# Where feed-forward weights begin in their buffers: eight places instead of one

## The chip, the cores and the metric

The kernel runs on one core of one Trainium2 chip. Its five engines (TensorE, VectorE, ScalarE, GpSimd and SyncE) run side by side and meet at semaphores. The metric is the time of one execution on the device, in microseconds; three executions before the change took 817.57, 817.77 and 818.57 us, with a median of 817.77 us.

## The reference

One encoder block on 512 tokens of width 1024, all in float32: three sub-layers, each with an RMSNorm before and after it and a residual.

```python
h = rms_norm(x, g_mix_pre);  proj = h @ w_in            # 1024 x 3080
...                                                     # two groups of 8 heads, joined, @ w_out
x = x + rms_norm(mix, g_mix_post)
ca = memory_cross_attention(rms_norm(x, g_mem_pre), rms_norm(mem, g_mem_kv), w_mem_q, w_mem_kv, w_mem_o)
x = x + rms_norm(ca, g_mem_post)
h = rms_norm(x, g_ffn_pre)
g, u = split(h @ w_gate_up)                             # 1024 x 2 * 2816
x = x + rms_norm((silu(g) * u) @ w_down, g_ffn_post)    # 2816 x 1024
```

The feed-forward part at the end is what the change concerns: 512 x 1024 by 1024 x 5632, then 512 x 2816 by 2816 x 1024.

## The kernel before, in words

Every float32 product is made of three matmuls of a rounded type. A matrix is split into `hi`, its rounded value, and `lo`, what the rounding lost, and `mm3` (L142 to L145) adds stationary hi by moving hi (L143), stationary hi by moving lo (L144) and stationary lo by moving hi (L145) in PSUM. The stationary operand is loaded into TensorE by its own instruction (LDWEIGHTS, the rows marked PEld), here 128 columns at a time; the moving operand streams past it, here up to 512 columns at a time.

The weights come in 63 units, listed in order at L200 to L222. `load_unit` (L102) brings one: SyncE issues a DMA into a buffer `raw` (L114, 128 x 1024 elements at a time, three buffers in turn), ScalarE casts it into `hi` (L118), and VectorE subtracts to get `lo` (L125; GpSimd does part of it for early units, L121). `unit` (L135) hands out the next unit and has the one after it loaded ahead. `hi` and `lo` have two buffers each, taken in turn, so the unit after next waits until TensorE has finished with its buffer. A unit is a tile of 128 partitions by `nkb` blocks by `ncol` columns, 8 x 256 or 4 x 512 elements of 4 bytes, 8192 bytes per partition. The opening stage uses the same buffers for `vhi264`, `vlo264` (8 blocks of 264 columns, 8448 bytes) and `vhi256`, `vlo256`. A scheduler orders the work by priorities, which `later` shifts.

The order of the stages is: value columns of the input projection (`v_products`, moving operand `vhi`/`vlo`, stationary `hTh`/`hTl`); the projections and the attention of four head groups; output projection with the keys and values of the memory; cross-attention; `w_mem_o`; and the feed-forward part.

Units 29 to 50 are the gate and up weights, in 11 pairs. There the weights are stationary, 128 columns at a time, and the normalised activations `fh`/`fl` are moving, 512 columns, for the first pair in two pieces of 256 columns. Each pair makes 128 x 512 results in PSUM for two blocks of gate (`ps_a`) and up (`ps_s`); ScalarE and VectorE turn them into `gh` and `gl` (L833 to L836). Units 51 to 62 are the down weights, six for each half of the 1024 output columns. There `gh`/`gl` are stationary and the weights are moving, 512 columns. Unit 56 is the last of the first half; it and unit 62 have two blocks instead of four. The second half's first unit, 57, takes the buffer of unit 55, which the end of the first half uses, so its cast and its subtraction come after that use.

Of the kernel before, what the change touches and what calls it, by code (L numbers as in the profile page):

```python
# [9 lines left out]
F32R = mybir.dt.float32r  # L10
# [4 lines left out]
P = 128  # L15
# [3 lines left out]
KB = D // P  # L19
# [14 lines left out]
def hybrid_block_kernel(  # L34
# [23 lines left out]
    wp = ctx.enter_context(tc.tile_pool(name="wp", bufs=2))  # L58
# [9 lines left out]
    def f32(ap):  # L68
        return ap.bitcast(F32)
# [32 lines left out]
    def load_unit(w, k0, nkb, c0, ncol, dst=None, sizes=None, after=None):  # L102
        u = len(loaded)
        if dst is None:
            hi = wp.tile([P, nkb, ncol], F32R, tag="hi", name=f"hi{u}", bufs=2)
            lo = wp.tile([P, nkb, ncol], F32R, tag="lo", name=f"lo{u}", bufs=2)
        else:
            hi, lo = dst()
        step = nkb if nkb * ncol <= 1024 else 4 if ncol < 512 else 2
        j = 0  # L110
        for n in sizes or [min(step, nkb - k) for k in range(0, nkb, step)]:
            raw = wp.tile([P, n, ncol], F32, tag="raw", name=f"raw{u}_{j}", bufs=3)
            r0 = (k0 + j) * P
            nc.sync.dma_start(  # L114
                raw,
                w[r0 : r0 + n * P, c0 : c0 + ncol].rearrange("(k p) n -> p k n", p=P),
            )
            act.copy(hi[:, j : j + n, :], raw)  # L118
            pk = 0 if j == 0 or not 0 <= u < 24 else 3 if ncol == 256 else 2 if u >= 18 else 0
            if pk:  # L120
                pool.tensor_tensor(  # L121
                    out=lo[:, j : j + pk, :], in0=raw[:, :pk, :], in1=f32(hi[:, j : j + pk, :]), op=ALU.subtract
                )
            if pk < n:
                dve.tensor_tensor(  # L125
                    out=lo[:, j + pk : j + n, :], in0=raw[:, pk:, :], in1=f32(hi[:, j + pk : j + n, :]), op=ALU.subtract
                )
            if after is not None:
                after(hi, lo, j, n)
            j += n  # L130
        loaded.append((hi, lo))
# [3 lines left out]
    def unit(ahead=1):  # L135
        n = used[0]
        used[0] += 1
        while len(loaded) < min(n + 1 + ahead, len(units)):
            load_unit(*units[len(loaded)])
        return loaded[n]  # L140
# [60 lines left out]
    for side in range(2):  # L201
        for g in fox_order if side == 0 else (0, 1):
            c = (0, 1544)[side] + 256 * g
            n = 264 if (side, g) == (0, 1) else 256
# [24 lines left out]
    with tc.tile_pool(name="mix", bufs=1, reuse_waits="tile") as bp:  # L229
# [403 lines left out]
        with later(-5):  # L633
            for half in range(2):
                hi, lo = unit()
# [10 lines left out]
    with tc.tile_pool(name="cross", bufs=1, reuse_waits="tile") as cp:  # L646
# [9 lines left out]
        with later(-115):  # L656
            for c in range(4):
                hi, lo = unit()
# [17 lines left out]
        for half in range(2):  # L676
            hi, lo = unit()
# [19 lines left out]
        for half in range(2):  # L697
            accs = [bank("a"), bank("a")]
            for k0 in (0, 4):
                hi, lo = unit()  # L700
# [15 lines left out]
        for h in range(4):  # L716
            hi, lo = unit()
# [11 lines left out]
            p = cp.tile([P, NT, NMEM], F32, tag="xp", name=f"xp{h}", bufs=2)  # L729
# [63 lines left out]
        for pair in range(2):  # L793
            for half, w in enumerate((w0, w1)):
                for t in (2 * pair, 2 * pair + 1):
                    acc = bank("a")
                    ts = slice(t * P, (t + 1) * P)
                    for k in range(KB):
                        hi, lo = w[k // 4]
# [11 lines left out]
    with tc.tile_pool(name="ffn", bufs=1, reuse_waits="tile") as fp:  # L811
# [30 lines left out]
        for half in range(2):  # L842
# [11 lines left out]
            for k0, n in groups[:4]:  # L854
                hi, lo = unit()
# [81 lines left out]
```

## Time and profile before

| what | value |
|---|---|
| median of three runs | 817.77 us (817.57 to 818.57) |
| the profiled execution | 817.99 us |
| its span, first to last instruction | 816.2 us |
| TensorE busy | 790.3 us, 97% of the span |
| VectorE, ScalarE, GpSimd busy | 54%, 46%, 14% |
| before 446 us | TensorE busy 427.03 us |
| 446 us to the end (370.20 us) | TensorE busy 363.32 us, VectorE 123.60, ScalarE 101.34 |
| mean granted TensorE clock | 0.997 |

In the profile's rows PE is TensorE's matmul, PEld its weight load, DVE VectorE, ACT ScalarE, POOL GpSimd, SP SyncE; L118 is line 118 of the kernel before. A row such as `ps_a<-fh,hi` names what is written and what is read. Matmuls overlap, so the duration of one is longer than the distance from its start to the next one's; where a price is wanted, the distance counts. The profiled execution's own time is 1.8 us more than its span.

### The profile page before, as it was taken

To read this page: it belongs to the slowest core of one execution; us is meant where nothing else is said; L and a number is where in the kernel's file an instruction comes from. 1 tells how busy PE (TensorE), PEld (TensorE's weight loads), DVE (VectorE), ACT (ScalarE), POOL (GpSimd) and SP (SyncE) were. 2 spreads that over 40 slices of the span, in tenths; PEclk is the share of its full clock that TensorE was granted. 3 is DMA by queue.
4 is the path that set the end of the run, shared out by engine and by line. 5 is a ranking of instruction groups with operands and counts; after the bars stand their busy time and mean duration, and the time that the engine had idled before them with its cause. 6 is when DMAs were issued, how large, how long until landed. Compare 5 with 4: busy or idle time off the path is not lost.

```text
span 816.2 us, 10512 instructions
## 1 busy us (share of the span) xinstructions
PE 790.3 (97%) x4040; PEld 660.2 (81%) x4040; DVE 437.5 (54%) x794; ACT 372.9 (46%) x679; POOL 117.3 (14%) x133
## 2 busy tenths in 40 slices
PE   7999999999999989999999999999999999999996
PEld 7876887887679867878787988888888888888885
DVE  6577889789887579554635433333333333113214
ACT  7357888567875257443436332232233323113111
POOL 6123233211324154100011000000000000000001
PEclk9999999999999999999999999999999999999999
DMA  6342113322314723412403033333333322232312
GB/s 235 90 118 62 42 53 104 104 78 78 104 52 134 254 97 126 138 52 78 141 16 104 26 104 104 103 104 104 104 104 104 95 88 85 94 103 73 111 50 104
DMA packets 60738, 79.91 MB, mean 98 GB/s; under 512 B 2704, under 2 KB 43664, under 8 KB 60688
## 3 DMA queue, kind: packets, MB, share of 16 engines
q1 hardware_dynamic: 59264, 74.49, 29.0%
q0 software_dynamic: 1280, 4.72, 1.7%
q8 instruction: 32, 0.52, 0.3%
q14 instruction: 18, 0.15, 0.1%
q10 hardware_dynamic: 144, 0.02, 0.0%
HBM read 77.13 MB, written 2.10 MB: 97 GB/s over the span
## 4 chain that ended last, share of the span: by engine, by line
PE 80%; DVE 6%; ACT 5%; issue 2%; POOL 2%; DMA 1%; DVEq 0%; POOLq 0%; ACTq 0%
PE ps_a L145 16%; PE ps_a L143 16%; PE ps_a L144 16%; PE ps_s L144 7%; PE ps_s L145 7%; PE ps_s L143 7%; PE ps_t L536 2%; DVE lo L125 2%; PE ps_o L545 1%; PE ps_o L143 1%; PE ps_t L145 1%; PE ps_t L144 1%; PE ps_s L517 1%; DVE p L533 1%; PE ps_o L144 1%
## 5 line engine op out<-in xcount | busy, mean ns | idle before, releaser
L125 DVE TENSOR_TENSOR lo<-raw,hi 128x1024 fp32r<-128x1024 f32 x118 | 145.2, 1255 | 143.1 <-ACT hi L118 141.9
L118 ACT CAST hi<-raw 128x1024 fp32r<-128x1024 f32 x122 | 124.3, 1048 | 182.0 <-PE ps_a L144 54.4
L143 PE MATMUL ps_a<-hTh,hi 128*128 128x512 f32 x192 | 76.6, 399 | 0.2 <-ACT hi L118 0.2
L145 PE MATMUL ps_a<-hTh,lo 128*128 128x512 f32 x192 | 76.1, 396 | 0.6 <-DVE lo L125 0.6
L144 PE MATMUL ps_a<-hTl,hi 128*128 128x512 f32 x192 | 75.6, 394 | 0.0
L143 PE MATMUL ps_s<-fh,hi 128*128 128x512 f32 (+1 forms) x192 | 71.6, 373 | 0.0
L144 PE MATMUL ps_s<-fl,hi 128*128 128x512 f32 (+1 forms) x192 | 71.6, 373 | 0.0
L145 PE MATMUL ps_s<-fh,lo 128*128 128x512 f32 (+1 forms) x192 | 71.5, 373 | 0.0
L144 PE MATMUL ps_a<-fl,hi 128*128 128x512 f32 (+1 forms) x192 | 71.5, 372 | 0.0
L145 PE MATMUL ps_a<-fh,lo 128*128 128x512 f32 (+1 forms) x192 | 71.5, 372 | 0.0
L143 PE MATMUL ps_a<-fh,hi 128*128 128x512 f32 (+1 forms) x192 | 71.4, 372 | 0.0
L834 DVE TENSOR_TENSOR silu<-silu,ps_s 128x512 f32<-128x512 f32 x22 | 15.1, 688 | 97.2 <-PE ps_s L145 97.2
L121 POOL TENSOR_TENSOR lo<-raw,hi 128x768 fp32r<-128x768 f32 (+1 forms) x20 | 44.9, 2243 | 96.8 <-ACT hi L118 93.9
L873 POOL TENSOR_TENSOR frs<-frs,mhalf 128x1 f32<-128x1 f32 x4 | 2.2, 546 | 356.1 <-DVE frs L872 356.1
L145 PEld LDWEIGHTS ps_a<-hTh,lo 128*128 128x128 f32 x192 | 36.1, 188 | 7.5 <-DVE lo L125 1.0
L144 PEld LDWEIGHTS ps_a<-fl,hi 128*128 128x128 f32 x192 | 36.2, 189 | 6.3
L143 PEld LDWEIGHTS ps_a<-hTh,hi 128*128 128x128 f32 x192 | 36.2, 188 | 6.4 <-ACT hi L118 0.4
L143 PEld LDWEIGHTS ps_s<-fh,hi 128*128 128x128 f32 x192 | 36.2, 189 | 6.2
L143 PEld LDWEIGHTS ps_a<-fh,hi 128*128 128x128 f32 x192 | 36.1, 188 | 6.3
L145 PEld LDWEIGHTS ps_s<-fh,lo 128*128 128x128 f32 x192 | 36.1, 188 | 6.2
L144 PEld LDWEIGHTS ps_s<-fl,hi 128*128 128x128 f32 x192 | 36.1, 188 | 6.2
L145 PEld LDWEIGHTS ps_a<-fh,lo 128*128 128x128 f32 x192 | 36.2, 188 | 6.1
(283 smaller groups left out, 1871.9 us busy)
## 6 DMA issues: line engine op xcount, KB each, us to landing
raw<-in_dram SPq DMA_DIRECT2D x126, 512.0 KB, 3.6
cb<-in_dram SPq DMA_DIRECT2D x8, 256.0 KB, 2.7
xo<-in_dram POOLq DMA_DIRECT2D x4, 512.0 KB, 7.1
out_dram<-yd SPq DMA_DIRECT2D x8, 256.0 KB, 2.0
rawv<-in_dram SPq DMA_DIRECT2D x3, 520.0 KB, 6.4
xt<-in_dram SPq DMA_DIRECT2D x3, 512.0 KB, 7.2
gb<-in_dram POOLq DMA_DIRECT2D x3, 512.0 KB, 4.0
mm<-in_dram POOLq DMA_DIRECT2D x1, 1024.0 KB, 6.0
```

The source lines that it names most:

```text
L118: act.copy(hi[:, j : j + n, :], raw)
L121: pool.tensor_tensor(out=lo[:, j : j + pk, :], in0=raw[:, :pk, :], in1=f32(hi[:, j : j + pk, :]), op=ALU.subtract)
L125: dve.tensor_tensor(out=lo[:, j + pk : j + n, :], in0=raw[:, pk:, :], in1=f32(hi[:, j + pk : j + n, :]), op=ALU.subtract)
L143: pe.matmul(dst, sh, mh, start=first, stop=False)
L144: pe.matmul(dst, sh, ml, start=False, stop=False)
L145: pe.matmul(dst, sl, mh, start=False, stop=last)
L517: pe.matmul(s[:, :w], q[:, h, ts], kt[:, h, :w], start=True, stop=False)
L533: dve.tensor_scalar(out=p[:, :n], in0=p[:, :n], scalar1=rs, scalar2=None, op0=ALU.mult)
L536: pe.transpose(tp[:, k * P : (k + 1) * P], p[:, k * P : (k + 1) * P], ident)
L545: pe.matmul(acc[:, a:], v[:, k, vh, :], m[:, k * PTS + a : k * PTS + SEQ], start=k == 0 and m is ph, stop=k == NT - 1 and m is pl,)
L834: dve.tensor_tensor(out=s, in0=s, in1=ua, op=ALU.mult)
L873: pool.tensor_tensor(out=r, in0=r, in1=mhalf[:, :1], op=ALU.pow)
```

## The change

A unit of `w_gate_up` or `w_down` no longer begins at the start of its `hi` and `lo` buffers but 8 x (u mod 8) elements of 4 bytes further on, where u is the unit's number: 0, 32, 64, ... 224 bytes. To hold that, the tile is a flat row of 8 x 256 + 56 elements, and the unit is a view of it with the same blocks and columns as before. Units of other weights keep offset zero, and unit 28, whose tiles come from another pool, isn't touched. No instruction is added, removed or moved on any engine.

```diff
     def load_unit(w, k0, nkb, c0, ncol, dst=None, sizes=None, after=None):
         u = len(loaded)
         if dst is None:
-            hi = wp.tile([P, nkb, ncol], F32R, tag="hi", name=f"hi{u}", bufs=2)
-            lo = wp.tile([P, nkb, ncol], F32R, tag="lo", name=f"lo{u}", bufs=2)
+            skip = 8 * (u % 8) if w in (w_gate_up, w_down) else 0
+
+            def place(name):
+                flat = wp.tile([P, KB * 256 + 56], F32R, tag=name, name=f"{name}{u}", bufs=2)
+                return flat[:, skip : skip + nkb * ncol].rearrange("p (k n) -> p k n", k=nkb)
+
+            hi, lo = place("hi"), place("lo")
         else:
             hi, lo = dst()
```

## The prediction

> **What bounds the kernel now.** I read the page first (span, busy shares, chain of waits), then the waits of TensorE in the stretch that the change reaches, then the stretches one by one, then single instructions in order of time.
>
> ```profile
> span 816.2 us, 10512 instructions
> ...
> PE 790.3 (97%) x4040; PEld 660.2 (81%) x4040; DVE 437.5 (54%) x794; ACT 372.9 (46%) x679; POOL 117.3 (14%) x133
> ...
> PE 80%; DVE 6%; ACT 5%; issue 2%; POOL 2%; DMA 1%; DVEq 0%; POOLq 0%; ACTq 0%
> ```
>
> TensorE is busy for 97% of the span and carries 80% of the chain that ended last. The edited addresses are used only by the feed-forward part, from its first product at about 446 us to the end, so the next view asks whom TensorE waited for after 440 us (columns: who waited, for whom, us in total, times, longest).
>
> ```profile
> engine line waited for: us in total, times, longest us
> PE ps_t L169 <- DVE fl L179: 0.4, 1, 0.4
> ```
>
> That is the whole list: one wait of 0.4 us, for an earlier stage's result. By stretch (length, then busy time and instruction count of each engine, the granted clock, the DMA share and rate):
>
> ```profile
> core 0: us, PE busy (x) PEld busy (x) DVE busy (x) ACT busy (x) POOL busy (x), PEclk, DMA share, GB/s
> 446.00:472.00 26.00, 25.52 (x214) 25.18 (x213) 12.77 (x23) 12.84 (x23) 2.56 (x3) 1.00 0.07 21
> 472.00:580.00 108.00, 108.00 (x478) 89.42 (x478) 37.45 (x41) 31.36 (x40) 0.00 (x0) 1.00 0.33 101
> 580.00:690.00 110.00, 110.00 (x487) 91.07 (x486) 37.12 (x41) 31.62 (x41) 0.00 (x0) 1.00 0.32 99
> 690.00:750.00 60.00, 60.00 (x266) 49.56 (x265) 14.54 (x15) 12.93 (x18) 0.00 (x0) 1.00 0.26 86
> 750.00:800.00 50.00, 49.93 (x221) 40.98 (x220) 14.57 (x17) 10.54 (x14) 0.55 (x1) 1.00 0.27 85
> ```
>
> From 472 to 750 us TensorE has no idle time at all, at the full granted clock of 1.00, while VectorE and ScalarE are busy for a third of it or less (37.45 and 31.36 of 108 us). So the feed-forward part lasts as long as its matmuls' spacing makes it, and casts, subtractions and loads lie beside them. What one of each takes between 476 and 690 us:
>
> ```profile
> L143 PE MATMUL ps_s<-fh,hi 128*128 128x512 f32 x160 | 62.2, 389 | 0.0
> ...
> L125 DVE TENSOR_TENSOR lo<-raw,hi 128x1024 fp32r<-128x1024 f32 x39 | 46.1, 1222 | 43.6 <-ACT hi L118 42.7
> L118 ACT CAST hi<-raw 128x1024 fp32r<-128x1024 f32 x40 | 40.1, 1048 | 68.7 <-PE ps_a L144 38.0 <-PE ps_s L144 29.5 <-DMA raw<-in_dram 1.2
> L143 PEld LDWEIGHTS ps_s<-fh,hi 128*128 128x128 f32 x160 | 30.1, 188 | 6.2
> ```
>
> A matmul's 389 ns is not its price, since matmuls overlap: the price is the distance from one start to the next.
>
> ```profile
> 496.44 0.39 PE L143 MATMUL ps_a<-fh,hi 128*128 128x512 f32 x1
> 496.44 0.19 PEld L144 LDWEIGHTS ps_a<-fl,hi 128*128 128x128 f32 x1
> ...
> 498.48 0.39 PE L143 MATMUL ps_a<-fh,hi 128*128 128x512 f32 x1
> ```
>
> Nine matmuls lie between the first and the last row: 2.04 us / 9 = 226.7 ns each. The weight load for the next matmul starts with the current one and ends 0.19 us later, inside that distance. The 256-column pieces of the first gate and up pair run closer together, and the rows of their weight loads show how close:
>
> ```profile
> 448.66 0.19 PEld L143 LDWEIGHTS ps_s<-fh,hi 128*128 128x128 f32 x1
> ...
> 449.62 0.19 PEld L145 LDWEIGHTS ps_s<-fh,lo 128*128 128x128 f32 x1
> ```
>
> Eight loads in 0.96 us are 120.0 ns from one to the next, although one lasts 0.19 us; loads overlap too. So a 512-column matmul leaves 226.7 - 120.0 = 107 ns of room for its weight load, and a 256-column matmul leaves none that this trace shows.
>
> **The change part by part.** *Where the tiles lie.* The new tile has 2048 + 56 = 2104 elements, and the buffers already have room for 8 x 264 = 2112, because the opening stage's `vhi264` and `vlo264` share them. So nothing grows, no other tile moves, and each engine keeps its instructions, their order and their waits. The stretch up to 446 us costs and gains nothing: its units keep an offset of zero. All buffers begin on a multiple of 256 bytes, and the earlier offsets inside them are multiples of 512 bytes; now a unit begins 32 x (u mod 8) bytes further on.
>
> *How many instructions are touched.* Units 29 to 50 are gate and up, 51 to 62 are down. Offset zero falls to units 32, 40, 48 and 56. Gate and up use the weights as the stationary operand: 192 matmuls of 256 columns for units 29 and 30 (offsets 160 and 192 bytes), and 17 x 48 = 816 of 512 columns in the other shifted units. Down uses them as the moving operand: 528 matmuls less the 24 of unit 56, so 504. Together 1512 matmuls get an operand that begins elsewhere.
>
> *The moving operand.* Before the change, the opening stage already has this case. `vhi264` holds blocks of 264 columns, 1056 bytes, so block k begins at 32 x k bytes past a 256-byte boundary, while `vhi256` beside it always begins on one, both against the same stationary `hTh` and `hTl`. Blocks 1, 2 and 3, each first 12 matmuls of 264 columns and then 12 of 256:
>
> ```profile
> 9.77 0.29 PE L143 MATMUL ps_s<-vhi,hTh 128*128 128x264 f32 x1
> ...
> 11.24 0.29 PE L143 MATMUL ps_a<-vhi,hTh 128*128 128x256 f32 x1
> ...
> 12.67 0.29 PE L143 MATMUL ps_s<-vhi,hTh 128*128 128x264 f32 x1
> ...
> 14.13 0.28 PE L143 MATMUL ps_a<-vhi,hTh 128*128 128x256 f32 x1
> ...
> 15.55 0.28 PE L143 MATMUL ps_s<-vhi,hTh 128*128 128x264 f32 x1
> ...
> 17.01 0.28 PE L143 MATMUL ps_a<-vhi,hTh 128*128 128x256 f32 x1
> ```
>
> The 264-column runs take 1.47, 1.46 and 1.46 us, 4.39 / 36 = 121.9 ns a matmul; the two 256-column runs between them take 1.43 and 1.42 us, 2.85 / 24 = 118.8 ns. The difference is 3.1 ns for 8 columns more. The two widths of above give (226.7 - 118.8) / 256 = 0.421 ns a column, so 8 columns are worth 3.4 ns, and 0.3 ns is left for the shifted start: a gain of 0.3 ns, where the rows' rounding of 0.01 us over 12 matmuls is worth 0.8. I take a gain of 0.2 ns. The upper bound is block 1 with 1.47 / 12 = 122.5 ns, which is 0.3 ns above 118.8 + 3.4 = 122.2. The lower bound is block 4, which begins 128 bytes past the boundary:
>
> ```profile
> 20.73 0.28 PE L144 MATMUL ps_s<-vlo,hTh 128*128 128x264 f32 x1
> ...
> 21.69 0.28 PE L143 MATMUL ps_a<-vhi,hTh 128*128 128x256 f32 x1
> ```
>
> Eight matmuls in 0.96 us, 120.0 ns each, are 2.2 ns under 122.2. These rows test the stationary side as well as far as a clash between the two streams goes, for what matters there is where one begins against the other.
>
> *The weight loads of gate and up.* A load that begins off a 256-byte boundary is not in this trace. From below its cost is nothing, or the same 2.2 ns of gain as above. From above I take the longest load of a feed-forward weight, which the next rows show beside the casts and subtractions (shortest, median, longest in ns):
>
> ```profile
> L143 PEld LDWEIGHTS ps_s<-fh,hi x192: 188/188/222, 448.7 to 688.7; 128*128 128x128 f32 x192
> ...
> L118 ACT CAST hi<-raw x62: 1039/1047/1055, 469.1 to 793.6; 128x1024 fp32r<-128x1024 f32 x62
> L125 DVE TENSOR_TENSOR lo<-raw,hi x62: 1215/1224/1227, 470.2 to 794.7; 128x1024 fp32r<-128x1024 f32 x62
> ```
>
> 222 - 188 = 34 ns more. Beside a 512-column matmul this is hidden, 120 + 34 = 154 ns against 226.7; without that cover the 816 loads would cost 28 us. In the 192 loads of units 29 and 30 it is not hidden: 192 x 34 ns = 6.5 us. I take zero, the nearest value by the moving operand's rows, since those reads show no price for a start at 32, 64 or 96 bytes.
>
> *The casts and subtractions.* Both write to the shifted places, and the subtraction and TensorE read from them. Their source `raw` already starts at 0, 64 or 128 bytes past a boundary, since its three buffers are 4160 bytes apart, and still 62 casts differ by 16 ns in all (1039 to 1055) and 62 subtractions by 12 (1215 to 1227). I take nothing; bounds are plus and minus 16 ns for each. Their cover is the idle two thirds of both engines. It is missing at one place, the start of down's second half, where the chain of waits leaves TensorE (start, length, what):
>
> ```profile
> 747.97 0.24 PE ps_o L145
> ...
> 748.24 1.06 ACT hi L118
> ...
> 749.32 1.23 DVE lo L125
> ...
> 750.60 0.50 PE ps_s L144
> ```
>
> Unit 57's cast and subtraction are 2.29 us on the path there, so this place is worth at most 2 x 16 ns by these bounds.
>
> *The DMAs* write `raw`, which doesn't move, and none is added.
>
> *Sum.* The profiled execution took 817.99 us, 1.8 around the span of 816.2, and lies 0.2 above the median of 817.77 and inside its range. 1512 x -0.2 ns = -0.3 us, the rest zero: **817.7 us**. With the moving operand's bounds, 1512 x -2.2 ns = -3.3 us and 1512 x 0.3 ns = 0.5 us, no change runs from 814.7 to 818.5.
>
> **The rivals.** *Fewer clashes, faster.* If the weight load and the moving read now meet in a worse pattern than they would at other offsets, all 1512 matmuls could gain what block 4 shows: 817.99 - 3.3 = 814.7 us. For it: a matmul of 512 columns at 0.421 ns each is 215.6 ns, and 226.7 - 215.6 = 11.1 ns is a fixed part of unknown origin. Against it: blocks 1 to 3, at three other offsets, gain nothing to speak of, and the spacing in the feed-forward part is the same whatever ScalarE and VectorE do. In the extreme the whole fixed part is a clash and goes: 1320 matmuls of 512 columns x 11.1 ns = 14.7 us, 803.3 us. The Trainium skill, in "TensorE: Matmul & The Clock Gate", section "Back-to-back issue gap", gives N / 2.4 + 2.5 ns for a warm matmul of N columns, 215.8 ns at 512; this trace disagrees by 10.9 ns, and if the offsets closed that gap the same 1320 matmuls would save 14.4 us.
>
> *Slower weight loads.* The 192 loads of units 29 and 30 stand 120.0 ns apart with matmuls at the same distance, so a longer occupation by the load goes straight to the end. At 34 ns more it is 6.5 us, 824.5 us. It decides (over 1.6 us) from 1.6 us / 192 = 8.5 ns a load. For it: these loads begin at 160 and 192 bytes, a case that nothing in this trace shows. Against it: reads of the moving operand at such places show no price.
>
> *A slower handover.* The 2.29 us of cast and subtraction before 750.60 us have no cover. If writing 32 bytes past a boundary doubled them, 817.99 + 2.3 = 820.3 us; it decides from 1.6 / 2.29 = 70% longer. Against it are the 16 and 12 ns of spread over three source offsets.
>
> *The shift does nothing at all.* hi and lo of a unit move together, so their relation stays as it is, and the time would be 818.0 us, which belongs to no change.
>
> **How the numbers follow.** A change of 0.2%, 1.6 us, is about what a measurement of this kernel can tell from none. No change has a chance of 0.79 (with the shift that does nothing), the faster rival 0.08 at 814.7 and 0.02 at 803.3, slower loads 0.08, the slower handover 0.03. So faster is 0.10, same 0.79 and slower 0.11, and the time is that of no change, 817.7 us. The range reaches down to 814.7, the end of the moving operand's bounds, and up to 820.3, the slower handover; outside lie the extreme gain and most of the slower loads, about 0.1 together.
>
> **What would show it.** Right: gate, up and down still have their starts 226.7 ns apart in all units, whatever u mod 8; units 29 and 30 still load every 120.0 ns; casts stay at 1039 to 1055 and subtractions at 1215 to 1227 ns; 472 to 750 us has no idle TensorE time. Wrong: a spacing that differs between shifted units and units 32, 40, 48 and 56 would make the address a price after all, below 226.7 for the faster rival. Unit 29's and 30's stretch from 446 to 472 us growing by more than 1.6 us would be the slower loads. A longer piece between 748.24 and 750.60 us would be the handover.

## The result: 1% slower, all of it in the distance between matmul starts

The changed kernel takes 826.03 us (825.93 to 827.10 in three runs) against 817.77 us, a ratio of 1.0102 with a 95% interval of 1.008 to 1.0125. The prediction was 817.7 us with a range of 814.7 to 820.3, so it missed by 8 us. Lines from L107 on have moved down by five in the changed kernel (L143 is L148, L118 is L123, L125 is L130).

The page of the changed kernel (span, busy time, chain of waits):

```profile
span 824.2 us, 10512 instructions
...
PE 797.9 (97%) x4040; PEld 659.8 (80%) x4040; DVE 437.9 (53%) x794; ACT 372.7 (45%) x679; POOL 117.7 (14%) x133
...
PE 80%; DVE 6%; ACT 5%; issue 2%; POOL 2%; DMA 1%; DVEq 0%; POOLq 0%; ACTq 0%
```

The span grew by 8.0 us. TensorE is busy 7.6 us longer, and its share of the chain is the same 80%. The waits of TensorE after 440 us (who waited, for whom, us, times, longest):

```profile
PE ps_t L174 <- DVE fl L184: 0.4, 1, 0.4
```

It is the one wait of 0.4 us from before, so nothing new is waited for. By stretch, in the columns of before:

```profile
446.00:472.00 26.00, 25.54 (x214) 25.13 (x214) 12.88 (x23) 13.00 (x24) 2.55 (x3) 1.00 0.05 21
472.00:580.00 108.00, 108.00 (x468) 87.58 (x467) 36.45 (x41) 31.15 (x40) 0.00 (x0) 1.00 0.33 98
580.00:690.00 110.00, 110.00 (x476) 89.08 (x475) 35.66 (x40) 29.95 (x39) 0.00 (x0) 1.00 0.32 96
690.00:750.00 60.00, 60.00 (x259) 48.34 (x258) 15.50 (x15) 12.14 (x16) 0.00 (x0) 1.00 0.31 97
750.00:800.00 50.00, 49.94 (x216) 40.00 (x215) 13.17 (x13) 11.24 (x14) 0.00 (x0) 1.00 0.26 84
```

TensorE is busy without a gap from 472 to 750 us, as before, at the full clock. But between 472 and 580 us it gets through 468 matmuls where it was 478, and between 580 and 690 us 476 where it was 487. One group of the same matmuls, then the casts and subtractions (shortest, median and longest in ns, first and last start), of the changed kernel:

```profile
L148 PEld LDWEIGHTS ps_a<-fh,hi x192: 187/188/193, 445.6 to 687.8; 128*128 128x128 f32 x192
...
L148 PE MATMUL ps_a<-fh,hi x192: 276/394/401, 445.8 to 688.0; 128*128 128x512 f32 x160, 128*128 128x256 f32 x32
...
L148 PE MATMUL ps_a<-hi,gh x66: 390/394/404, 694.4 to 751.0; 128*128 128x512 f32 x66
...
L123 ACT CAST hi<-raw x62: 1035/1048/1055, 469.0 to 801.0; 128x1024 fp32r<-128x1024 f32 x62
L130 DVE TENSOR_TENSOR lo<-raw,hi x62: 1216/1224/1227, 470.1 to 802.1; 128x1024 fp32r<-128x1024 f32 x62
...
L148 PE MATMUL ps_t<-hi,gh x44: 388/394/400, 756.4 to 817.0; 128*128 128x512 f32 x44
```

Casts (1035 to 1055 ns) and subtractions (1216 to 1227) are where they were, and so are the weight loads (median 188). What changed is when the first down matmul starts, 694.4 us, where this row of before has 689.6, with the same start of the stage at 445.8 or 445.9:

```profile
L143 PE MATMUL ps_a<-fh,hi x192: 280/389/396, 445.9 to 683.4; 128*128 128x512 f32 x160, 128*128 128x256 f32 x32
...
L143 PE MATMUL ps_a<-hi,gh x66: 389/389/389, 689.6 to 744.6; 128*128 128x512 f32 x66
...
L143 PE MATMUL ps_t<-hi,gh x44: 388/389/393, 749.9 to 809.0; 128*128 128x512 f32 x44
```

So gate and up lost 4.8 us. The first matmul on `ps_t`, which belongs to down's second half, starts at 756.4 us where it was 749.9, and the last at 817.0 where it was 809.0: down lost 1.7 and 1.5 us more.

How the loss lies among the units is read from single starts. A pair's matmuls come in runs of 24: gate, up, gate, up, so its two units take turns. In the changed kernel, the first matmul of four successive runs of 24 (timeline, start and duration in us):

```profile
482.76 0.39 PE L148 MATMUL ps_a<-fh,hi 128*128 128x512 f32 x1
...
488.35 0.39 PE L148 MATMUL ps_s<-fh,hi 128*128 128x512 f32 x1
...
493.80 0.39 PE L148 MATMUL ps_a<-fh,hi 128*128 128x512 f32 x1
...
499.39 0.40 PE L148 MATMUL ps_s<-fh,hi 128*128 128x512 f32 x1
```

The first run is unit 31, begun 224 bytes past a boundary: 5.59 us / 24 = 233 ns a matmul. The second is unit 32, at offset zero, right behind it on the same engine: 5.45 / 24 = 227 ns. The third, unit 33 at 32 bytes, takes 233 again. The mean distance from one start to the next within each unit, worked out from the trace's starts without the change-overs (in gate and up, the first two distances of each run of 24 are left out), is this (ns, 512 columns; before, every unit has 226.7):

| bytes past the boundary | 0 | 32 | 64 | 96 | 128 | 160 | 192 | 224 |
|---|---|---|---|---|---|---|---|---|
| gate and up: weights stationary | 226.7 | 233.3 | 233.4 | 234.3 | 233.0 | 233.3 | 228.9 | 233.2 |
| down: weights moving | (unit 56, too short) | 233.4 | 228.9 | 233.4 | 232.9 | 234.3 | 233.4 | 233.2 |

Units with the same offset agree within 0.1 ns in gate and up. The second row read backwards is nearly the first: 192 stationary and 64 moving both cost 2.2 ns, 96 stationary and 160 moving both 7.6. Moving 64 bytes puts the two starts 64 apart in the other sense, and -64 and 192 differ by 256; that is why the distance is counted modulo 256 bytes below. Within a unit the distances repeat in a short cycle rather than being equal; unit 33 begins 

```
231 229 235 232 235 232 235 231 235 232 235 232 235 231 235 232 235 ...   (ns from start to start)
```

while a unit at zero repeats 226, 227, 227.

### The profile page after: what moved, and what is told of

It is laid out like the page before. It is cut to its first block, busy times and chain, and to the rows that moved or that the text cites. A ratio compares the mean times of both kernels' runs of the same rounds, so it can differ in the third digit from the quotient of the medians.

```text
span 824.2 us, 10512 instructions
## 1 busy us (share of the span) xinstructions
PE 797.9 (97%) x4040; PEld 659.8 (80%) x4040; DVE 437.9 (53%) x794; ACT 372.7 (45%) x679; POOL 117.7 (14%) x133
## 4 chain that ended last, share of the span: by engine, by line
PE 80%; DVE 6%; ACT 5%; issue 2%; POOL 2%; DMA 1%; DVEq 0%; POOLq 0%; ACTq 0%
PE ps_a L150 16%; PE ps_a L148 16%; PE ps_a L149 16%; PE ps_s L149 7%; PE ps_s L150 7%; PE ps_s L148 7%; PE ps_t L541 2%; DVE lo L130 2%; PE ps_o L550 1%; PE ps_o L148 1%; PE ps_t L149 1%; PE ps_t L150 1%; DVE p L538 1%; PE ps_o L149 1%; PE ps_s L522 1%
## 5 line engine op out<-in xcount | busy, mean ns | idle before, releaser
L130 DVE TENSOR_TENSOR lo<-raw,hi 128x1024 fp32r<-128x1024 f32 x118 | 145.2, 1254 | 148.1 <-ACT hi L123 146.7
L123 ACT CAST hi<-raw 128x1024 fp32r<-128x1024 f32 x122 | 124.2, 1047 | 186.2 <-PE ps_a L149 55.9
L148 PE MATMUL ps_a<-hTh,hi 128*128 128x512 f32 x192 | 76.5, 399 | 0.1
L148 PE MATMUL ps_a<-fh,hi 128*128 128x512 f32 (+1 forms) x192 | 72.3, 377 | 0.0
L148 PE MATMUL ps_s<-fh,hi 128*128 128x512 f32 (+1 forms) x192 | 72.1, 375 | 0.0
L148 PEld LDWEIGHTS ps_a<-fh,hi 128*128 128x128 f32 x192 | 36.1, 188 | 7.3
L148 PEld LDWEIGHTS ps_s<-fh,hi 128*128 128x128 f32 x192 | 36.1, 188 | 6.8
L148 PEld LDWEIGHTS ps_a<-hTh,hi 128*128 128x128 f32 x192 | 36.2, 188 | 6.4 <-ACT hi L123 0.3
```

The source lines that it names most:

```text
L130: dve.tensor_tensor(out=lo[:, j + pk : j + n, :], in0=raw[:, pk:, :], in1=f32(hi[:, j + pk : j + n, :]), op=ALU.subtract)
L148: pe.matmul(dst, sh, mh, start=first, stop=False)
```

## The experiments

The theory after this reading, called the relation theory below: what costs is where the moving read begins against where the weight load begins, modulo 256 bytes. Its rivals: the boundary theory, that any operand of TensorE off a 256-byte boundary costs; and the write theory, that ScalarE's and VectorE's writes to shifted places collide with TensorE's reads. All edits are to the changed kernel. Where a run has one execution, its time alone is worth about 1 us: gate and up, with the same work before them, begin anywhere from 445.6 to 447.2 us in these runs. There the distances within the stage carry the reading.

### Both operands shifted by the same 96 bytes

```diff
-            skip = 8 * (u % 8) if w in (w_gate_up, w_down) else 0
+            skip = 24 if w in (w_gate_up, w_down) else 0
...
-        fh = ox.tile([P, KB, SEQ], F32R, tag="x1", name="fh")
+        fh = ox.tile([P, KB * SEQ + 64], ...)[:, 24 : 24 + KB * SEQ].rearrange("p (k n) -> p k n", k=KB)
+        # and so fl, gh, gl
```

> Every feed-forward weight unit begins 96 bytes past a multiple of 256, and so do fh, fl, gh and gl, the operands that they meet; everything else is as in the changed kernel. Relation theory (what costs is the distance between where the moving read and the weight load begin, modulo 256 bytes): the distance is zero again, all 512-column starts stand 226.7 ns apart, and the time is that of before, 817.8 us, ratio 0.999 to 1.001. Boundary theory (any operand of TensorE that begins off a 256-byte boundary costs): at least the 233 to 234 ns of the changed kernel in every unit, 826 us or more, since no unit is left at zero. Write theory (casts and subtractions that write to shifted places collide with TensorE's reads): also 826 us or more.

Measured: 818.21 us against 818.11 on the same chip, ratio 1.000 (0.999 to 1.0009). Its stretches:

```profile
472.00:580.00 108.00, 108.00 (x480) 89.51 (x480) 38.05 (x42) 31.59 (x41) 0.00 (x0) 1.00 0.33 99
580.00:690.00 110.00, 110.00 (x487) 91.09 (x486) 36.95 (x40) 31.15 (x40) 0.00 (x0) 1.00 0.32 100
690.00:750.00 60.00, 60.00 (x266) 49.55 (x265) 14.11 (x15) 12.79 (x18) 0.00 (x0) 1.00 0.28 87
```

478 matmuls between 472 and 580 us have become 480, and every unit is at 226.7 ns again, but for a few distances at the start of unit 31 and at the handover in unit 57, as before, though no operand of the feed-forward matmuls begins on a boundary. That excludes the boundary theory and the write theory. The distance between the two operands is what counts, here at 96 bytes.

### The moving operand of gate and up shifted by 32 bytes, weights as in the change

```diff
-        fh = ox.tile([P, KB, SEQ], F32R, tag="x1", name="fh")
+        fh = ox.tile([P, KB * SEQ + 64], ...)[:, 8 : 8 + KB * SEQ].rearrange("p (k n) -> p k n", k=KB)
+        # and so fl
```

> The changed kernel, with fh and fl (the moving operands of gate and up) begun 32 bytes past a boundary, while the weight units keep their eight places; down is left as in the changed kernel. Relation theory: the row of spacings by unit moves on by one step. Units at 32 bytes (33, 41, 49) take 226.7 ns and those at 0 (32, 40, 48) take the 233.2 that 224 bytes took; 64 takes 233.3, 96 takes 233.4, 128 takes 234.3, 160 takes 233.0, 192 takes 233.3, and 224 (31, 39, 47) takes the 228.9 of 192; the time stays within 1 us of 826. Boundary theory: no gate or up unit at 226.7 ns, those at 0 bytes at 233 for the moving operand's sake, the others as before or worse. Write theory: units as in the changed kernel, 226.7 ns for 32, 40 and 48.

Measured: 827.01 us in one execution. The first matmuls of successive runs of 24 in its timeline, from unit 32's on:

```profile
478.53 0.40 PE L148 MATMUL ps_s<-fh,hi 128*128 128x512 f32 x1
...
484.12 0.39 PE L148 MATMUL ps_a<-fh,hi 128*128 128x512 f32 x1
...
489.62 0.39 PE L148 MATMUL ps_s<-fh,hi 128*128 128x512 f32 x1
...
495.22 0.39 PE L148 MATMUL ps_a<-fh,hi 128*128 128x512 f32 x1
...
500.66 0.39 PE L148 MATMUL ps_s<-fh,hi 128*128 128x512 f32 x1
```

Unit 32, at zero, now takes (484.12 - 478.53) / 24 = 233 ns, unit 31 (second run) (489.62 - 484.12) / 24 = 229 and unit 33, at 32 bytes like fh, (500.66 - 495.22) / 24 = 227. By unit, with the expectation in brackets: 0 bytes 233.2 (233.2), 32: 226.7 (226.7), 64: 233.4 (233.3), 96: 233.3 (233.4), 128: 234.3 (234.3), 160: 232.4 (233.0), 192: 233.3 (233.3), 224: 228.9 (228.9). The row moved on by one step, as the relation theory has it, and only at 160 is it off by more than 0.1. The boundary theory wanted no gate or up unit at 226.7, and the write theory wanted unit 32 to stay there; both fail again. The down units stayed where they were.

### Gate and up alone, and down alone

```diff
-            skip = 8 * (u % 8) if w in (w_gate_up, w_down) else 0
+            skip = 8 * (u % 8) if w is w_gate_up else 0      # the other run: w is w_down
```

> The shift for gate and up units alone (stationary operand); down begins at zero. By the changed kernel's spacings: 20 units of 48 matmuls with 104.8 ns of excess over 226.7 summed over units, 5.0 us, less 0.2 us for the 256-column pair: 822.6 us, with down at 226.7 ns throughout. If instead down's moving reads carry the loss, 818 us.

> The shift for down units alone (moving operand); gate and up begin at zero. By the changed kernel's spacings 3.2 us more than before: 821.0 us, gate and up at 226.7 ns throughout. The two parts alone should add up to the 8.3 us of both; a sum that falls short by over 1 us would mean that the two stages share a cause that is not the spacing.

Measured: 822.96 us for gate and up alone, ratio 1.0056 (1.0039 to 1.0072), and 821.19 us for down alone, ratio 1.0031 (1.0018 to 1.0044), against 818.11. That is 4.85 and 3.08 us, where 822.6 and 821.0 us were expected, and 7.9 together, where both at once cost 8.3; the untouched stage keeps 226.7 ns in each. The whole loss is the sum of the matmuls' longer distances, and each stage pays its own.

### Distances finer than 32 bytes

```diff
+FINE = {31: 1, 32: 2, 33: 3, 34: 4, ...}                     # elements of 4 bytes, by unit
-            skip = 8 * (u % 8) if w in (w_gate_up, w_down) else 0
+            skip = FINE.get(u, 0)
```

> Each feed-forward unit has a distance of its own, most not a multiple of 32: gate and up units 31 to 50 begin 4, 8, 12, 16, 20, 24, 28, 36, 40, 48, 56, 80, 112, 144, 176, 188, 208, 240, 248 and 252 bytes past a boundary, units 29 and 30 (256 columns) 208 and 16; down units 51 to 55 begin 4, 8, 16, 24 and 28 past it, 57 to 61 at 48, 60, 204, 240 and 252. Step theory (the two reads meet by steps of 32 bytes): 4 to 28 bytes cost nothing, 226.7 ns, and 36 to 60 cost the 233.3 of 32. Smooth theory (the cost grows with the distance): from 226.7 at 4 up to 233 at 28, and down again from 240 to 252. Third theory (zero is best only among multiples of 32): some unit comes in under 226.7 ns, and a faster kernel can be made of it; 5 ns less in a unit would be worth 7 us over all feed-forward matmuls of 512 columns. The time is between 818 and 827 us by all three.

Measured: 825.49 us against 818.62 for the kernel before, one execution of each. The mean distances in ns:

| stationary, bytes | 4 | 8 | 12 | 16 | 20 | 24 | 28 | 36 | 40 | 48 | 56 | 80 | 112 | 144 | 176 | 188 | 208 | 240 | 248 | 252 |
|---|---|---|---|---|---|---|---|---|---|---|---|---|---|---|---|---|---|---|---|---|
| ns | 232.4 | 230.7 | 229.7 | 233.3 | 233.2 | 231.1 | 235.1 | 234.0 | 233.3 | 233.3 | 233.3 | 232.0 | 233.3 | 233.5 | 230.0 | 233.3 | 232.7 | 226.9 | 233.4 | 226.7 |

| moving, bytes | 4 | 8 | 16 | 24 | 28 | 48 | 60 | 204 | 240 | 252 |
|---|---|---|---|---|---|---|---|---|---|---|
| ns | 237.7 | 233.5 | 231.8 | 234.0 | 228.8 | 233.3 | 228.4 | 231.2 | 233.4 | 230.2 |

All three theories of this run fall. There are no steps of 32 bytes (4 bytes already cost 5.7 ns), there is no smooth rise, and nothing is under 226.7. Two starts other than zero, 240 and 252 stationary, also reach it. Nor is the distance the whole story at this grain: 252 stationary and 4 moving are the same distance, and take 226.7 and 237.7. The relation theory holds for steps of 32 bytes, where it was tested; what the finer pattern follows is open.

### hi and lo apart

```diff
+HI = {31: 8, 32: 16, ...}; LO = {41: 8, 42: 16, ...}         # elements, by unit
             def place(name):
+                skip = (HI if name == "hi" else LO).get(u, 0)
```

> hi and lo of a unit apart: units 31 to 40 shift hi by 32, 64, 96, 128, 160, 192, 224, 16, 48 and 8 bytes and leave lo at zero, 41 to 50 shift lo by the same and leave hi; down units 51 to 55 shift hi by 32, 64, 96, 128 and 192, and 57 to 61 shift lo. Theory of the overlapping load (a matmul is held back by the weight load that runs beside it, the next matmul's): in gate and up two of three loads are of hi and one is of lo, so hi alone costs two thirds of the 6.6 ns, 231.1 ns at 32 bytes, and lo alone one third, 228.9. Theory of the own load (a matmul is held back by its own weights' place): the same thirds in the mean, but the slow matmuls are those on hi (L148, L149) or on lo (L150) themselves and not the ones before them. Theory of the pair hi to lo (their distance from each other matters): the same cost for both, whichever is shifted.

Measured: 825.12 us in one execution. Over the ten offsets hi alone takes 226.9 to 233.5 ns, 231.1 in the mean, and lo alone 226.7 to 233.3, 231.5 in the mean (at 32 bytes 231.9 and 233.2). Hi alone at 32 bytes comes near the 231.1 that the theory of the overlapping load gave, but lo alone, one load in three, loses as much, and not the 228.9 expected; the thirds fall. Nor do the two parts add up: 16 bytes cost next to nothing on hi alone (226.9) or on lo alone (226.7), and 6.6 ns on both together (233.3 in the run before). The theory of the pair, which also gave equal costs, cannot be the cause, since in the changed kernel hi and lo share their place and lose all the same. A reading that would fit, and that no run here shows, is that one matmul's delay sets where the next load meets its stream, so that a unit has to be taken as a cycle. This run doesn't tell the overlapping load from the matmul's own.

### 256 columns, and 384 with 128

```diff
-            for piece in ((0, 256), (256, 512)) if u == 0 else ((0, 512),):
+            for piece in ((0, 256), (256, 512)):                         # e7; in e8, for u > 0: (0, 384), (384, 512)
```

> The changed kernel with all gate and up units in two pieces of 256 columns, as units 29 and 30 always were; twice as many matmuls, each with its own weight load. Cover theory (where weight loads themselves set the distance of 120 ns, a shifted start costs nothing): 117 to 121 ns in every unit, whatever its place, and about 960 x (240 - 226.7) ns = 12.8 us more than a kernel at zero, near 833 us with down's loss of 3. Theory without cover (each matmul pays for its own distance): 123 to 127 ns in shifted units, 838 us or more.

> The changed kernel with gate and up units 31 to 50 in a piece of 384 and one of 128 columns. At zero distance (units 32, 40, 48) 384 columns should stand about 226.7 - 128 x 0.417 = 173 ns apart. Fixed theory (a clash costs the same for every load): 179 to 181 ns in shifted units, as 6.6 ns more at 512. Theory by length (the cost grows with the streamed columns beyond the 120 ns that a load takes): half as much, 176 ns. Pieces of 128 columns stand 120 ns apart in all units. The time is near 890 us.

Measured: 837.43 and 878.11 us, one execution of each. With 256 columns, unit 32, at zero, and unit 34, at 64 bytes, from the first matmul of a run of 24 to the first of the next:

```profile
487.85 0.28 PE L148 MATMUL ps_s<-fh,hi 128*128 128x256 f32 x1
...
490.72 0.28 PE L148 MATMUL ps_a<-fh,hi 128*128 128x256 f32 x1
...
511.04 0.28 PE L148 MATMUL ps_s<-fh,hi 128*128 128x256 f32 x1
...
513.76 0.28 PE L148 MATMUL ps_a<-fh,hi 128*128 128x256 f32 x1
```

That is 2.87 / 24 = 119.6 ns at zero and 2.72 / 24 = 113.3 ns at 64 bytes. With 384 columns, unit 31, at 224 bytes, and then unit 32, at zero:

```profile
471.53 0.34 PE L148 MATMUL ps_a<-fh,hi 128*128 128x384 f32 x1
...
475.78 0.33 PE L148 MATMUL ps_s<-fh,hi 128*128 128x384 f32 x1
...
479.94 0.34 PE L148 MATMUL ps_a<-fh,hi 128*128 128x384 f32 x1
```

4.25 / 24 = 177 ns against 4.16 / 24 = 173. The mean distances of all units, by how many columns stream, with the changed kernel's 512 columns beside them (change-overs and waits left out):

| columns | units at zero | shifted units | shifted less zero |
|---|---|---|---|
| 128 | 111.7 | 111.6 to 111.7 | -0.1 to 0.0 |
| 256 | 119.7 | 114.1 to 119.9 | -5.6 to 0.2 |
| 384 | 173.3 | 173.2 to 176.8 | -0.1 to 3.5 |
| 512 | 226.7 | 228.9 to 234.3 | 2.2 to 7.6 |

These are the runs that explain the miss. At 512 columns zero is the fastest of the eight places, at 384 it shares that, at 256 it is among the slowest (64 bytes gives about 114 ns in two units, 117.9 in a third), and at 128 the place makes no difference. The fixed theory is refuted by the 384 columns. The theory by length isn't borne out either: 128, 160 and 224 bytes cost the 3 ns or so that it gave (176.0 to 176.8 ns), but 32, 96 and 192 bytes cost under 0.5. Of the two theories for 256 columns, the one with cover is right on spacings (117 to 121 expected, 114.1 to 119.9 found), but its picture of a flat 120 isn't, since shifted units run below it. The time of the 256-column kernel isn't explained by the spacings, which give 817.8 + 960 x (2 x 118.4 - 226.7) ns + 3.2 us = 831 us. Most of the 6 us left is at ten waits of TensorE for subtractions, 2.8 us of idle time, which this kernel's trace shows and the changed kernel's doesn't: among the starts of gate and up are 23 distances of over 200 ns, all at these waits or within a few matmuls of them, 5.7 us above 118 ns each in all. For 384 and 128 the same sum, 817.8 + 960 x (175 + 111.7 - 226.7) ns + 3.2, gives 878.6 us, and 878.11 was measured. The 890 expected had taken 120 ns for 128 columns, where 111.7 came.

### A shift where it should help

```diff
+APART = {4: 48, 7: 48, 12: 16, 13: 16, 14: 16, 15: 16, 29: 16, 30: 16}   # elements; all other units 0
-            skip = 8 * (u % 8) if w in (w_gate_up, w_down) else 0
+            skip = APART.get(u, 0)
```

> All units at zero as before, but for eight whose matmuls stream 256 columns: the memory key units 12 to 15 and the first gate and up units 29 and 30 (stationary) begin 64 bytes past a boundary, the value units 4 and 7 (moving) 192 bytes past it, which is the same distance. All 512-column matmuls are left at distance zero. Width theory (at 256 columns zero is the slowest distance, 119.7 ns against 114.1 to 117.9 at 64 bytes, as at 512 columns it is the fastest): 576 matmuls gain 1.8 to 5.6 ns each, 1.0 to 3.2 us, 815 to 817 us, ratio 0.996 to 0.999, and spacings of 256 columns under 118 ns in these stages. Cover theory (weight loads set the distance of 120 ns in these stages whatever the place): no change, ratio 1.000, spacings stay at 119 to 120.

Measured: 816.22 us against 817.98, ratio 0.9982 (0.9973 to 0.9991), 1.8 us under the kernel before. In the first gate and up pair the weight loads show the distance of 256 columns, which was 120.0 ns (timeline):

```profile
460.21 0.19 PEld L149 LDWEIGHTS ps_a<-fh,hi 128*128 128x128 f32 x1
...
461.91 0.19 PEld L149 LDWEIGHTS ps_s<-fh,hi 128*128 128x128 f32 x1
```

Fifteen loads in 1.70 us are 113.3 ns each. From its first matmul to the first of 512 columns this pair takes 25.1 us, where it took 26.1: 1.0 of the 1.8 us. In the key units the median distance fell from 120 to 114 ns, and in the value units, which come in four stretches, from 120 to between 114 and 118. The width theory holds, near the middle of what it expected.

### A weight load that doesn't walk

```diff
-                                acc[:, piece[0] : piece[1]], wh_[:, k, cs], wl_[:, k, cs],
+                                acc[:, piece[0] : piece[1]], still_col(wh_[:, k, cs]), still_col(wl_[:, k, cs]),
+    def still_col(w): return w[:, 0:1].to_broadcast([P, P])
```

> The changed kernel, with gate and up's weights read from one column: the stationary operand of each matmul is the first column of its block of 128, repeated 128 times, so that the weight load reads one place instead of walking through 512 bytes; it computes other values, the feed-forward part is not the reference's. The matmuls, their number and the moving reads are the same. Two-walk theory (the loss comes from two reads that walk through the memory at different paces, and the places where they meet): no walk, no dependence on the unit's place; all gate and up units within 1 ns of each other, at or under 226.7. Start theory (only the place where the load begins counts): shifted units still at 233 to 234, units 32, 40 and 48 at 226.7. Down is as in the changed kernel, 3.2 us.

Measured: 824.6 us in one execution. Successive runs of 24 in its timeline, units 31, 32, 31, 32:

```profile
471.13 0.39 PE L148 MATMUL ps_a<-fh,hi 128*128 128x512 f32 x1
...
476.67 0.39 PE L148 MATMUL ps_s<-fh,hi 128*128 128x512 f32 x1
...
482.22 0.39 PE L148 MATMUL ps_a<-fh,hi 128*128 128x512 f32 x1
...
487.77 0.39 PE L148 MATMUL ps_s<-fh,hi 128*128 128x512 f32 x1
...
493.31 0.39 PE L148 MATMUL ps_a<-fh,hi 128*128 128x512 f32 x1
```

The runs take 5.54 to 5.55 us each: 231.1 ns in all 20 units of 512 columns, whatever their place. So the start theory falls: with the load reading one place, nothing depends on where the unit begins. But the other half of the expectation was wrong as well, since 231.1 ns is between the good and the bad distances and not at 226.7. The loads' own rows last 188 ns in the mean, as in the changed kernel, so it isn't a longer row that shows. Two reads that walk from the same place are better than one that stands still; why, this run doesn't show.

## Why the prediction was wrong, step by step

*What bounds the kernel* was right: TensorE's spacing from 472 us on, with all else beside it. The changed kernel shows it by having no new wait and 8 us more.

*Where the tiles lie* was right: nothing else moved. The count of 1512 matmuls was right too, 1320 of them of 512 columns.

*The moving operand* is the step that failed. It took the price of a shifted start from matmuls of 264 and 256 columns, 0.2 ns of gain with bounds of -2.2 and +0.3, and carried it over to 512 columns. The rows weren't misread: at 256 columns a shift costs nothing or helps, by up to 5.6 ns. But the effect changes sign with the width, and at 512 columns it is a loss of 2.2 to 7.6 ns: 1.7 and 1.5 us in down's halves and 4.8 in gate and up, so about 6 ns for each of the 1320 shifted matmuls of 512 columns, where the sum had a gain of 0.2. The rows were an extrapolation over a factor of two in the streamed length, and the bounds were drawn as if they weren't. The price per column of 0.421 ns, from the same two widths, gave no sign of it: from 384 to 512 columns it is (226.7 - 173.3) / 128 = 0.417, but from 256 to 384 it is (173.3 - 119.7) / 128 = 0.419 and from 128 to 256 only (119.7 - 111.7) / 128 = 0.06, so a matmul of 256 columns sits near where something other than its columns sets the distance; what that is, these runs don't show.

*The weight loads* were taken at zero because the moving rows showed nothing, and fell with them. The remark that those rows test the stationary side as well was right at steps of 32 bytes, where the two rows of the table mirror each other; between them it fails (4 bytes moving takes 237.7 ns, 252 stationary 226.7).

*The casts, subtractions and DMAs* were right: 1035 to 1055 and 1216 to 1227 ns after, inside the bounds of 16 ns. The handover at down's second half, in the changed kernel's chain, still takes 1.06 and 1.24 us:

```profile
754.71 1.06 ACT hi L123
...
755.79 1.24 DVE lo L130
```

*The rivals.* That it matters where the weight load begins against the moving read was right, but stood only as a way to gain: a better offset was looked for, and that zero might already be the best one was not. The slower weight loads had the right sign and the wrong place: they priced units 29 and 30, of 256 columns, and called the 512-column matmuls covered by 107 ns of room. Units 29 and 30 lost nothing (window 446 to 472 us: 214 matmuls before and after), and the covered ones lost everything. Room for a longer load was no cover here: the loads' median stayed at 188 ns, and the distances grew all the same. The handover did not happen. The sentence on what would show the prediction wrong, a spacing that differs between shifted units and units 32, 40, 48 and 56, named what came, with the sign that it didn't expect.

The quoted rule of the Trainium skill, 215.8 ns for a warm matmul of 512 columns ("TensorE: Matmul & The Clock Gate", section "Back-to-back issue gap"), which the section gives for an isolated matmul, was reached at no distance: no feed-forward unit of 512 columns has a mean under 226.5 ns in any run here, so none of the offsets tried removes the 11 ns above it.

## What to carry to other kernels

Where float32 matmuls stood back to back with a weight load each, the place where the stationary operand begins against the moving one, modulo 256 bytes, was part of the price, though no wait, load or cast showed it; count matmuls per stretch, or take start-to-start distances by unit. Keep long moving reads (512 columns) and their weights at the same place, as the kernel before had them, and try 64 bytes apart where 256 columns stream. A price read at one width is no price at another: bound it again where the width differs.

## What the runs showed of the hardware that I had not expected

- The distance between operand starts moves a 512-column matmul from 226.7 to as much as 237.7 ns (4 bytes, moving). Both operands 96 bytes off a boundary cost nothing.
- At 256 columns the order turns round: 119.7 ns at zero, 113.3 at 64 bytes in the run that used it. At 128 columns it is 111.7 ns at every place.
- A stationary operand that is one column repeated takes 231.1 ns at every place, longer than a walking read from the same place as the moving one.
- Matmuls of 512 columns at a bad distance settle into a repeating cycle of spacings, in gate and up with the same mean for units with the same offset to 0.1 ns.
- Why these meetings cost what they cost (which parts of the memory clash, if any) no run here shows.
